# Sums of rank-times-key products on TensorE instead of VectorE, in the routing stage of a hybrid encoder layer

## The chip, the cores and the metric

The kernel runs on one core of one Trainium2 chip. The metric is the device time of one execution in microseconds (us); lower is better. The core has five engines with one queue each: TensorE (PE in the profile, its weight loads PEld), VectorE (DVE), ScalarE (ACT), GpSimd (POOL) and SyncE (SP), which here only issues DMAs. Each engine takes the instructions of its queue in order.

## The reference

One encoder layer on 512 tokens of width 1024. A mixer (a gated linear recurrence and a convolution side by side, then an output projection) is followed by PEER, a retrieval over 128 x 128 single-neuron experts; the change lies in PEER's routing alone:

```python
q = jnp.einsum("td,de->te", xt, w_q)                 # 8 heads x 2 halves x 128
s = jnp.einsum("thpc,hpkc->thpk", q, sub_keys)       # scores against 128 keys per half
s1, i1 = lax.top_k(s[:, :, 0], 16)
s2, i2 = lax.top_k(s[:, :, 1], 16)
cand_s = s1[..., :, None] + s2[..., None, :]         # 16 x 16 sums
cand_i = i1[..., :, None] * 128 + i2[..., None, :]
top_s, pos = lax.top_k(cand_s, 16)
idx = jnp.take_along_axis(cand_i, pos, axis=-1)
gate = jax.nn.softmax(top_s, axis=-1)
act = jax.nn.gelu(jnp.einsum("thkd,td->thk", expert_u[idx], xt))
out = jnp.einsum("thk,thkd->td", gate * act, expert_v[idx])
```

## The kernel before

After the mixer the kernel has four blocks of 128 tokens. Three of them are served densely: for all experts the products with `expert_u` are formed in 128 steps (`dense_u`, 24 matmuls of 384 columns each, lines 478 to 480), gates are scattered into a dense table, and the products with `expert_v` are summed in 128 steps (line 777). The fourth block gathers its experts' rows by indirect DMAs.

**The routing stage** lies between the mixer and the scatter of the gates, from about 270 to 480 us of the span. It loops over `hp`, 16 half heads. For each it runs a query (`query`, 24 matmuls of 512 columns, lines 587 to 589, evicted by ScalarE at line 591), the scores (line 602, evicted by ScalarE to a tile `s` at line 606) and, on VectorE, the sixteen best of each of the four token blocks (`rank`, by `best16`, lines 504 to 508). The queries run one step ahead. The list `US` says how many `dense_u` steps stand behind each `hp`: they fill TensorE while VectorE ranks; five of them stand behind the last one. Their weights are split into a high and a low part by ScalarE (line 108) and GpSimd or VectorE (line 110).

**`choose`** runs after `hp` = 3, 7 and 11 for two heads each and after 13 and 15 for one head each; with four token blocks that is m = 8 or m = 4. It converts the ranks' indices (`ii`, line 525, ScalarE), forms the candidate sums (line 529, GpSimd for m = 8), takes their sixteen best, turns the positions into the two indices j of the candidates (`pa`, `pf`, `pb`, lines 543 to 550), and looks up the keys' numbers without a gather: `eq` (line 554) is one where j equals a rank, [128, 2, 16 ranks, 16m] in bf16; line 557 multiplies it by the keys `ii`; four additions (three at line 560, the last at line 562) sum over the sixteen ranks into `key_d`. The gates go by GpSimd and ScalarE (lines 564 to 569).

**The order on each engine** is written when the program is built: the framework's scheduler places an instruction on its engine at the time at which it expects its inputs, by its own estimate of each duration, and takes the earlier one of the program first where several are ready. On the chip the engine then keeps that order, whatever comes late. After the last `choose` come `eidx` (line 614), transposes of the gates and keys (line 638) and the scatter (`hot`, `oa`, lines 661 and 665 on VectorE, `p_g`, line 671 on TensorE), in which VectorE also splits the weights of more `dense_u` steps.

Of the kernel before, what the change touches and what calls it, by code (L numbers as in the profile page):

```python
# [8 lines left out]
F32 = mybir.dt.float32  # L9
F32R = mybir.dt.float32r  # L10
BF16 = mybir.dt.bfloat16
# [7 lines left out]
P = 128  # L19
T = 512  # L20
D = 1024
NB = T // P
# [3 lines left out]
K = 16  # L26
NK = 128
# [33 lines left out]
def tile_kernel(ctx, tc, x, par, wi, bd, kd, mg, wo, wq, keys, u_rows, v_rows, u_t, v_t, fg, ffg, sel, out):  # L61
    nc = tc.nc
# [4 lines left out]
    ident = keep.tile([P, P], F32, name="ident")  # L67
# [4 lines left out]
    gate_d = keep.tile([P, H, NB, K], F32, name="gate_d")  # L72
    key_d = keep.tile([P, 2, H, NB, K], F32, name="key_d")
# [27 lines left out]
    def load(src):  # L101
        t = raw.tile([P, D], F32, name="raw_t")
        nc.sync.dma_start(t, src)
        return t

    def split(t, eng, pool=wp):
        hi = pool.tile([P, D], F32R, name="w_hi")
        nc.scalar.copy(hi, t)  # L108
        lo = pool.tile([P, D], F32R, name="w_lo")
        eng.tensor_sub(lo, t, f(hi))  # L110
        return hi, lo
# [33 lines left out]
    with ExitStack() as mx:  # L145
# [11 lines left out]
        with ExitStack() as m1:  # L157
# [169 lines left out]
            for n, eb in enumerate(order):  # L327
# [17 lines left out]
                kind, j = divmod(eb, 4)  # L345
# [47 lines left out]
            for b in range(NB):  # L393
                t = hb.tile([P, D], F32, name="h_t")
# [98 lines left out]
    for _ in range(4):  # L493
        t = gp.tile([P, D], F32, name="g_t")
# [4 lines left out]
    lp = ip.enter_context(tc.tile_pool(name="lp", bufs=1, side="right"))  # L499
    ioj = lp.tile([P, K, K * RM], BF16, name="ioj")  # L500
    nc.gpsimd.iota(ioj, pattern=[[1, K], [0, K * RM]], base=0, channel_multiplier=0, allow_small_or_imprecise_dtypes=True)

    def best16(val, idx, src, scratch):
        nc.vector.max(val[:, 0:8], src)
        nc.vector.max_index(idx[:, 0:8], val[:, 0:8], src)
        nc.vector.match_replace(scratch, val[:, 0:8], src, -3.4028235e38)
        nc.vector.max(val[:, 8:16], scratch)
        nc.vector.max_index(idx[:, 8:16], val[:, 8:16], scratch)

    def rank(rp, v, i, src):  # L510
        s2 = rp.tile([P, NK], F32, name="s2")
        best16(v, i, src, s2)

    def merge(t):
        return t.rearrange("p h b k -> p (h b) k")

    def choose(rp, v, i, g, keys_, h0, n):

        hh = slice(h0, h0 + n)
        vv = v[:, hh].rearrange("p h b t k -> p (h b) t k")  # L520
        m = vv.shape[1]
        shp = [P, m, K]

        ii = rp.tile([P, 2, K, m], BF16, name="ii")
        nc.scalar.copy(ii, i[:, hh].rearrange("p h b t k -> p t k (h b)"))

        cs = rp.tile([P, m, NCD], F32, name="cs", bufs=1)
        for lo_, ni, nj, c0 in ((0, 4, K, 0), (4, 12, 4, 64)):
            (nc.gpsimd if n > 1 else nc.vector).tensor_tensor(
                cs[:, :, c0:c0 + ni * nj].rearrange("p h (i j) -> p h i j", j=nj),  # L530
                vv[:, :, 0, lo_:lo_ + ni].unsqueeze(3).to_broadcast([P, m, ni, nj]),
                vv[:, :, 1, 0:nj].unsqueeze(2).to_broadcast([P, m, ni, nj]), op=ALU.add)
        ts = rp.tile(shp, F32, name="ts")
        pos = rp.tile(shp, U32, name="pos")
        for h in range(m):
            c2 = rp.tile([P, NCD], F32, name="c2")
            best16(ts[:, h], pos[:, h], cs[:, h], c2)

        pa = rp.tile([P, 5, m, K], U32, name="pa")
        for q, (op, arg) in enumerate(((ALU.logical_shift_right, 4), (ALU.logical_shift_right, 2),  # L540
                                       (ALU.bitwise_and, 15), (ALU.bitwise_and, 12),
                                       (ALU.logical_shift_right, 6))):
            nc.vector.tensor_scalar(pa[:, q], pos, arg, None, op0=op)
        pf = rp.tile([P, 5, m, K], F32, name="pf")
        nc.scalar.copy(pf, pa)
        pb = rp.tile([P, 2, K, m], BF16, name="pb")
        pbm = pb.rearrange("p t k m -> p t m k")
        nc.vector.scalar_tensor_tensor(pbm[:, 0], pf[:, 1], -12.0, pf[:, 0], op0=ALU.add, op1=ALU.max)
        nc.vector.tensor_mul(pf[:, 3], pf[:, 3], pf[:, 4])
        nc.vector.tensor_sub(pbm[:, 1], pf[:, 2], pf[:, 3])  # L550

        eq = rp.tile([P, 2, K, K * m], BF16, name="eq", bufs=1)
        shp2 = [P, 2, K, K * m]
        nc.vector.tensor_tensor(eq, pb.rearrange("p t k m -> p t (k m)").unsqueeze(2).to_broadcast(shp2),
                                ioj[:, :, 0:K * m].unsqueeze(1).to_broadcast(shp2), op=ALU.is_equal)
        e4 = eq.rearrange("p t j (k m) -> p (t j) k m", m=m)
        nc.vector.tensor_tensor(e4, e4, ii.rearrange("p t j m -> p (t j) m").unsqueeze(2).to_broadcast([P, 2 * K, K, m]),
                                op=ALU.mult)
        for w in (8, 4, 2):
            nc.vector.tensor_add(eq[:, :, 0:w], eq[:, :, 0:w], eq[:, :, w:2 * w])  # L560
        e1, e2 = (eq[:, :, w].rearrange("p t (k m) -> p t k m", m=m) for w in range(2))
        nc.vector.tensor_add(keys_[:, :, hh].rearrange("p t h b k -> p t k (h b)"), e1, e2)
        g = merge(g[:, hh])
        nc.gpsimd.tensor_tensor(g, ts, ts[:, :, 0:1].to_broadcast(shp), op=ALU.subtract)
        nc.scalar.activation(g, g, AF.Exp)
        den = rp.tile([P, m], F32, name="den")
        nc.vector.tensor_reduce(den, g, axis=AX.X, op=ALU.add)
        nc.vector.reciprocal(den, den)
        nc.gpsimd.tensor_tensor(g, g, den.unsqueeze(2).to_broadcast(shp), op=ALU.mult)

    with ExitStack() as rt:
        kp = rt.enter_context(tc.tile_pool(name="kp", bufs=1, side="right"))
        ky = kp.tile([P, 16, NK], F32, name="ky")
        nc.sync.dma_start(ky, keys)
        rp = rt.enter_context(tc.tile_pool(name="rp", bufs=2, side="right"))
        qp = rt.enter_context(tc.tile_pool(name="qp", bufs=4, side="right"))
        ps_q = rt.enter_context(tc.tile_pool(name="ps_q", bufs=3, space=PSUM))
        ps_s = rt.enter_context(tc.tile_pool(name="ps_s", bufs=3, space=PSUM))
        v16 = kp.tile([P, H, NB, 2, K], F32, name="v16")
        i16 = kp.tile([P, H, NB, 2, K], U32, name="i16")  # L580

        def query(hp):
            hi, lo = split(load(wq[hp].rearrange("p c e -> p (c e)")), nc.gpsimd)
            pq = ps_q.tile([P, T], F32, name="pq")
            for c in range(NC):
                cs = slice(c * P, (c + 1) * P)
                nc.tensor.matmul(pq, hi[:, cs], m_hi[:, c, :], start=(c == 0), stop=False)  # L587
                nc.tensor.matmul(pq, hi[:, cs], m_lo[:, c, :], start=False, stop=False)  # L588
                nc.tensor.matmul(pq, lo[:, cs], m_hi[:, c, :], start=False, stop=(c == NC - 1))  # L589
            q = qp.tile([P, T], F32, name="q", bufs=2)  # L590
            nc.scalar.activation(q, pq, AF.Copy)
            return q

        for _ in range(EARLY):
            dense_u(len(us), nc.gpsimd)
        qs = [query(0)]
        for hp in range(16):
            if 0 < hp < 15:
                qs.append(query(hp + 1))
            p = ps_s.tile([P, NB, NK], F32, name="p_s")  # L600
            for b in range(NB):
                nc.tensor.matmul(p[:, b, :], qs[hp][:, b * P:(b + 1) * P], ky[:, hp, :], start=True, stop=True)
            if hp == 0:
                qs.append(query(1))
            s = qp.tile([P, NB, NK], F32, name="s")
            nc.scalar.activation(s, p, AF.Copy)
            for b in range(NB):
                rank(rp, v16[:, hp // 2, b, hp % 2], i16[:, hp // 2, b, hp % 2], s[:, b])
            for _ in range(US[hp]):
                dense_u(len(us), nc.gpsimd)  # L610
            for h0, n in ((0, 2), (2, 2), (4, 2), (6, 1), (7, 1)):
                if hp == 2 * (h0 + n) - 1:
                    choose(rp, v16, i16, gate_d, key_d, h0, n)
        nc.vector.scalar_tensor_tensor(eidx, key_d[:, 0, :, DB], float(NK), key_d[:, 1, :, DB], op0=ALU.mult, op1=ALU.add)
    ip.close()

# [179 lines left out]
    for i in range(NK):  # L796
        n, o = divmod(i + AHEAD_W, GQ)
# [8 lines left out]
        if i < NK - LAST:  # L806
            w = ws.pop(i)
# [85 lines left out]
```

## Time and profile before

| what | value |
|---|---|
| median of three runs | 1543.34 us (1542.52 to 1551.58) |
| the profiled execution | 1543.64 us, span of its instructions 1541.5 us |
| mean granted clock of TensorE in it | 0.978 of 2.4 GHz |
| busy: TensorE, VectorE, ScalarE, GpSimd | 1467.7, 1232.5, 626.7, 625.4 us |

The span runs from the first to the last instruction. The rows below give times in us from the span's start. Matmuls overlap, so the busy time of TensorE is not its time at full rate; the distance from one start to the next is.

### The profile page before, as it was taken

How to read it: one execution, taken by the hardware profiler on the slowest of the kernel's cores; microseconds unless marked ns; L12 is line 12 of the kernel's file. 1: busy time of each engine (PE TensorE's matmuls, PEld its weight loads, DVE VectorE, ACT ScalarE, POOL GpSimd, SP SyncE). 2: the span in 40 equal slices, each digit the busy share in tenths (PEclk: the TensorE clock that was granted, in tenths of full speed). 3: DMA queues.
4: the chain of work that ended last, by engine and by line, in shares of the span. 5: the costliest groups of instructions: out<-in, count | busy, mean ns of one | idle time of the engine just before them, and what ended most of it. 6: DMA issues, size and time to landing. Idle time of an engine off the chain costs nothing.

```text
span 1541.5 us, 21654 instructions
## 1 busy us (share of the span) xinstructions
PE 1467.7 (95%) x7939; PEld 1289.4 (84%) x7939; DVE 1232.5 (80%) x2267; ACT 626.7 (41%) x926; POOL 625.4 (41%) x378
## 2 busy tenths in 40 slices
PE   5998698999988999999999999999999999999997
PEld 4766467899977899898999999999999999888886
DVE  5998556599999999937777777777777778788887
ACT  5457633344434555433333333333333333333333
POOL 1636542467551000124545545544454444443330
PEclk8999899999998999999999999999999999999999
DMA  6211313233222665588899898999989899889983
GB/s 238 82 55 58 134 69 123 97 109 98 92 95 100 226 212 213 212 259 311 290 334 318 327 340 289 342 305 332 326 318 326 301 348 319 304 310 339 331 290 135
DMA packets 137787, 358.69 MB, mean 233 GB/s; under 512 B 10064, under 2 KB 59472, under 8 KB 134352
## 3 DMA queue, kind: packets, MB, share of 16 engines
q1 hardware_dynamic: 100240, 222.03, 42.0%
q0 software_dynamic: 36864, 134.23, 24.2%
q8 instruction: 62, 1.02, 0.3%
q10 hardware_dynamic: 576, 1.05, 0.2%
q14 instruction: 45, 0.37, 0.1%
HBM read 327.91 MB, written 29.36 MB: 232 GB/s over the span
## 4 chain that ended last, share of the span: by engine, by line
PE 81%; DVE 13%; ACT 3%; issue 1%; POOL 1%; DMA 0%; SPq 0%; DVEq 0%; ACTq 0%; POOLq 0%
PE po L777 34%; PE p_e L478 10%; PE p_e L479 10%; PE p_e L480 10%; PE p_g L671 3%; DVE oa L665 2%; PE pq L587 2%; PE pq L588 2%; PE pq L589 2%; DVE hot L661 1%; PE pz L432 1%; PE pz L431 1%; PE pz L433 1%; PE pz L339 1%; PE pz L340 1%
## 5 line engine op out<-in xcount | busy, mean ns | idle before, releaser
L108 ACT CAST w_hi<-raw_t 128x1024 fp32r<-128x1024 f32 x302 | 315.9, 1050 | 411.6 <-PE p_e L479 266.8
L478 PE MATMUL p_e<-m_hi,w_hi 128*128 128x384 f32 x1024 | 350.7, 342 | 4.4 <-ACT w_e L487 3.5
L480 PE MATMUL p_e<-m_hi,w_lo 128*128 128x384 f32 x1024 | 347.3, 339 | 0.0
L479 PE MATMUL p_e<-m_lo,w_hi 128*128 128x384 f32 x1024 | 346.8, 339 | 0.3 <-DVE m_lo L142 0.3
L110 POOL TENSOR_TENSOR w_lo<-raw_t,w_hi 128x1024 fp32r<-128x1024 f32 x70 | 189.8, 2720 | 349.2 <-ACT w_hi L108 349.2
L110 DVE TENSOR_TENSOR w_lo<-raw_t,w_hi 128x1024 fp32r<-128x1024 f32 x232 | 280.9, 1222 | 13.6 <-ACT w_hi L108 13.4
L693 POOL DMA_INDIRECT g_t<-in_u_rows,eidx x128 | 197.4, 1543 | 214.0 <-DVE g_t L705 170.2
L693 POOL DMA_INDIRECT g_t<-in_v_rows,eidx x128 | 178.7, 1396 | 234.8 <-DVE acc L715 222.1
L777 PE MATMUL po<-w_hi,wt_hi 128*128 128x512 f32 x768 | 240.6, 393 | 0.0
L777 PE MATMUL po<-w_hi,wt_lo 128*128 128x512 f32 x768 | 239.5, 391 | 0.0
L777 PE MATMUL po<-w_lo,wt_hi 128*128 128x512 f32 x768 | 238.8, 390 | 0.0
L478 PEld LDWEIGHTS p_e<-m_hi,w_hi 128*128 128x128 f32 x1024 | 194.5, 190 | 8.3 <-ACT w_e L487 3.9
L479 PEld LDWEIGHTS p_e<-m_lo,w_hi 128*128 128x128 f32 x1024 | 194.5, 190 | 3.5 <-DVE m_lo L142 0.5
L480 PEld LDWEIGHTS p_e<-m_hi,w_lo 128*128 128x128 f32 x1024 | 194.5, 190 | 0.0
L777 PEld LDWEIGHTS po<-w_lo,wt_hi 128*128 128x128 f32 x768 | 144.2, 188 | 32.9
L777 PEld LDWEIGHTS po<-w_hi,wt_lo 128*128 128x128 f32 x768 | 144.3, 188 | 30.5
L705 DVE SCALAR_TENSOR_TENSOR g_t<-g_t,Xg 128x1024 f32<-128x1024 f32 x128 | 152.0, 1222 | 19.0 <-DMA g_t<-in_u_rows,eidx 18.8
L777 PEld LDWEIGHTS po<-w_hi,wt_hi 128*128 128x128 f32 x768 | 143.2, 188 | 24.9
L715 DVE SCALAR_TENSOR_TENSOR acc<-g_t,dots,acc 128x1024 f32<-128x1024 f32 x127 | 162.5, 1279 | 1.7 <-DMA g_t<-in_v_rows,eidx 1.7
L750 ACT CAST wt_hi<-w_f 128x384 fp32r<-128x384 f32 x69 | 35.4, 513 | 182.1 <-PE po L777 182.1
L752 DVE TENSOR_TENSOR wt_lo<-w_f,wt_hi 128x384 fp32r<-128x384 f32 x69 | 38.5, 558 | 73.7 <-ACT wt_hi L750 73.6
L665 DVE TENSOR_TENSOR oa<-hot,trb 128x1024 bf16<-128x1024 bf16 x144 | 92.3, 699 | 0.6
(220 smaller groups left out, 1906.2 us busy)
## 6 DMA issues: line engine op xcount, KB each, us to landing
raw_t<-in_u_t SPq DMA_DIRECT2D x128, 512.0 KB, 6.1
raw_t<-in_v_t SPq DMA_DIRECT2D x128, 512.0 KB, 6.1
scr_g<-stg SPq DMA_DIRECT2D x24, 1024.0 KB, 4.8
g_s<-scr_g SPq DMA_DIRECT2D x16, 1536.0 KB, 14.6
raw_t<-in_wi SPq DMA_DIRECT2D x16, 512.0 KB, 4.2
raw_t<-in_wq SPq DMA_DIRECT2D x16, 512.0 KB, 3.6
raw_t<-in_wo SPq DMA_DIRECT2D x8, 512.0 KB, 3.6
raw_t<-in_kd SPq DMA_DIRECT2D x6, 512.0 KB, 3.5
```

Source lines behind the costliest of these rows:

```text
L108: nc.scalar.copy(hi, t)
L110: eng.tensor_sub(lo, t, f(hi))
L478: nc.tensor.matmul(p, hi[:, cs], m_hi[:, c, :TD], start=(c == 0), stop=False)
L479: nc.tensor.matmul(p, hi[:, cs], m_lo[:, c, :TD], start=False, stop=False)
L480: nc.tensor.matmul(p, lo[:, cs], m_hi[:, c, :TD], start=False, stop=(c == NC - 1))
L665: nc.vector.tensor_tensor(oa[:, q], hot[:, 1], over(2 + q, 1), op=ALU.mult)
L671: nc.tensor.matmul(p[:, t, :], hot[:, 0, g, :, o], oa[:, q, g, :, o], start=(q == 0), stop=(q == 2))
L693: nc.gpsimd.indirect_dma_start(out=t, out_offset=None, in_=rows, in_offset=bass.IndirectOffsetOnAxis(ap=eidx[:, k // K, k % K:k % K + 1], ...
L705: nc.vector.scalar_tensor_tensor(t, t, 1.0, Xg, op0=ALU.mult, op1=ALU.mult, accum_out=dots[:, k:k + 1])
L715: nc.vector.scalar_tensor_tensor(acc, t, dots[:, k:k + 1], acc, op0=ALU.mult, op1=ALU.add)
L752: weighed.append(nc.vector.tensor_sub(wlo, flat(w), f(whi)))
L777: nc.tensor.matmul(po[b][hf], lhs[:, bs], rhs[:, hf * 512:(hf + 1) * 512], start=(i == 0 and n == 0), stop=(i == NK - 1 and n == 2))
```

## The change

The three halving additions and the last addition of `choose` go. In their place TensorE sums the sixteen products: sixteen matmuls with a bf16 unit matrix `identb` as one operand and `eq[:, :, j]`, two by 16m columns, as the other, accumulated in a tile of the scores' PSUM pool (`p_s`, three buffers), which VectorE then copies to `key_d`. `identb` is copied once from the f32 unit matrix by ScalarE. The conversion `ii` moves from ScalarE to VectorE. The tile `s` of evicted scores has six buffers instead of four.

```diff
+    identb = lp.tile([P, P], BF16, name="identb")
+    nc.scalar.copy(identb, ident)
...
-    def choose(rp, v, i, g, keys_, h0, n):
+    def choose(rp, ps, v, i, g, keys_, h0, n):
...
-        nc.scalar.copy(ii, i[:, hh].rearrange("p h b t k -> p t k (h b)"))
+        nc.vector.tensor_copy(ii, i[:, hh].rearrange("p h b t k -> p t k (h b)"))
...
-        for w in (8, 4, 2):
-            nc.vector.tensor_add(eq[:, :, 0:w], eq[:, :, 0:w], eq[:, :, w:2 * w])
-        e1, e2 = (eq[:, :, w].rearrange("p t (k m) -> p t k m", m=m) for w in range(2))
-        nc.vector.tensor_add(keys_[:, :, hh].rearrange("p t h b k -> p t k (h b)"), e1, e2)
+        pk = ps.tile([P, NB, NK], F32, name="p_s")[:, 0:2, 0:K * m]
+        for j in range(K):
+            nc.tensor.matmul(pk, identb, eq[:, :, j], start=(j == 0), stop=(j == K - 1))
+        nc.vector.tensor_copy(keys_[:, :, hh].rearrange("p t h b k -> p t k (h b)"), pk.rearrange("p t (k m) -> p t k m", m=m))
...
-            s = qp.tile([P, NB, NK], F32, name="s")
+            s = qp.tile([P, NB, NK], F32, name="s", bufs=6)
...
-                    choose(rp, v16, i16, gate_d, key_d, h0, n)
+                    choose(rp, ps_s, v16, i16, gate_d, key_d, h0, n)
```

## Rows read from the trace of the kernel before

**Rows 1.** The page, busy time of each engine, us, share of the span and instructions.

```profile
PE 1467.7 (95%) x7939; PEld 1289.4 (84%) x7939; DVE 1232.5 (80%) x2267; ACT 626.7 (41%) x926; POOL 625.4 (41%) x378
```

**Rows 2.** Chain of waits, 390 to 425 us: start, length, engine, tile, line.

```profile
396.80 0.89 PE p_s L602 x8
398.71 0.48 DVE v L504 x2
```

**Rows 3.** Windows: engines' busy us (instructions), granted clock, DMA share, GB/s.

```profile
420.00:440.00 20.00, 20.00 (x113) 18.67 (x112) 20.00 (x61) 3.47 (x5) 12.02 (x4) 1.00 0.32 106
440.00:450.00 10.00, 2.61 (x14) 2.29 (x13) 9.50 (x54) 5.97 (x10) 4.08 (x4) 0.85 0.16 52
```

**Rows 4.** Timeline of TensorE: start, length, line, shape, [idle before and its releaser].

```profile
411.13 0.39 PE L589 MATMUL pq<-m_hi,w_lo 128*128 128x512 f32 x1
...
437.44 0.42 PE L478 MATMUL p_e<-m_hi,w_hi 128*128 128x384 f32 x1
...
441.54 0.34 PE L480 MATMUL p_e<-m_hi,w_lo 128*128 128x384 f32 x1
449.27 2.07 PE L602 MATMUL p_s<-ky,q 128*128 128x128 f32 x8 [7.39 <-ACT q L591]
...
468.56 0.69 PE L478 MATMUL p_e<-m_hi,w_hi 128*128 128x384 f32 x1 [3.55 <-ACT w_e L487]
...
480.75 0.33 PE L638 MATMUL p_e<-ident,src 128*128 128x128 f32 x1 [0.95 <-ACT src L637]
```

**Rows 5.** Timeline of ScalarE, around the first, third and fourth choose.

```profile
311.20 0.59 ACT L591 ACTIVATE q<-pq 128x512 f32<-128x512 f32 x1
...
316.81 0.31 ACT L565 ACTIVATE gate_d<-gate_d 128x128 f32<-128x128 f32 x1 [3.23 <-POOL gate_d L564]
...
413.71 0.31 ACT L565 ACTIVATE gate_d<-gate_d 128x128 f32<-128x128 f32 x1 [5.03 <-POOL gate_d L564]
...
415.05 0.59 ACT L591 ACTIVATE q<-pq 128x512 f32<-128x512 f32 x1
...
441.62 0.42 ACT L525 CAST ii<-i 128x128 bf16<-128x128 uint32 x1 [13.12 <-DVE i L508]
...
448.63 0.59 ACT L591 ACTIVATE q<-pq 128x512 f32<-128x512 f32 x1
```

**Rows 6.** Groups by line on VectorE, 278 to 482 us: busy us, mean ns | idle before.

```profile
L560 DVE TENSOR_TENSOR eq<-eq 128x1024 bf16<-128x1024 bf16 (+3 forms) x15 | 29.4, 1959 | 0.1
...
L562 DVE TENSOR_TENSOR key_d<-eq 128x256 f32<-128x256 bf16 (+1 forms) x5 | 4.6, 922 | 0.0
```

**Rows 7.** Groups by line and shape on VectorE, 200 to 500 us: a read from PSUM.

```profile
L142 DVE TENSOR_TENSOR m_lo<-pt,m_hi 128x512 fp32r<-128x512 f32 x8 | 5.3, 688 | 5.6 <-ACT m_hi L141 5.6
```

**Rows 8.** Timeline of TensorE at the start of the scatter: bf16 matmuls of 128 columns.

```profile
489.78 1.55 PE L671 MATMUL p_g<-oa,hot 128*128 128x128 bf16 x24
```

**Rows 9.** Timeline of VectorE: three products of line 557, the last rank, `eidx`.

```profile
419.31 4.29 DVE L557 TENSOR_TENSOR eq<-eq,ii 128x4096 bf16<-128x4096 bf16 x1
...
449.91 3.27 DVE L557 TENSOR_TENSOR eq<-eq,ii 128x2048 bf16<-128x2048 bf16 x1
...
461.57 0.47 DVE L504 MAX8 v<-s 128x8 f32<-128x128 f32 x2
...
475.12 1.23 DVE L557 TENSOR_TENSOR eq<-eq,ii 128x2048 bf16<-128x2048 bf16 x1
...
480.32 0.29 DVE L614 SCALAR_TENSOR_TENSOR eidx<-key_d 128x128 int32<-128x128 f32 x1
```

**Rows 10.** Timeline of GpSimd beside the first of these products.

```profile
417.19 14.83 POOL L110 TENSOR_TENSOR w_lo<-raw_t,w_hi 128x1024 fp32r<-128x1024 f32 x4 [1.83 <-ACT w_hi L108]
```

**Rows 11.** Short windows after waits of TensorE, columns as in Rows 3.

```profile
468.00:469.00 1.00, 0.43 (x1) 0.44 (x2) 1.00 (x9) 0.98 (x3) 0.80 (x1) 0.50 0.00 0
...
474.00:475.00 1.00, 1.00 (x7) 1.00 (x6) 1.00 (x1) 0.99 (x3) 0.00 (x0) 0.86 0.00 0
...
485.00:490.00 5.00, 5.00 (x27) 4.52 (x26) 5.00 (x8) 0.56 (x1) 0.00 (x0) 0.71 0.13 49
```

## The prediction

> **What bounds the kernel now.** The page comes first: TensorE is busy for 95% of the span [rows 1], so a gain can only come from time in which it stands or runs at the lower of its two clocks. Next, windows over the routing stage [rows 3]. From 420 to 440 us TensorE and VectorE are both busy all the time, TensorE at clock 1.00. From 440 to 450 TensorE is busy for 2.6 us and VectorE for 9.5. Third, the chain of waits [rows 2]: it runs through TensorE up to the scores at 396.80 and from 398.71 through VectorE. So VectorE's savings before 396.80 are worth nothing, and from there they count only until TensorE is the later one again. Last, the timelines. TensorE finishes a `dense_u` step at about 441.7 and then stands for 7.39 us before the last scores, which wait for a query that ScalarE evicts at 448.63 [rows 4, 5]. ScalarE was held up by `ii`, for which it waited 13.12 us on VectorE's ranks [rows 5]. TensorE stands for another 3.55 us before 468.56 and reaches the first transpose of the scatter at 480.75 [rows 4]. The stage ends there, and from there on VectorE's and TensorE's work are what they were. The change is therefore priced by when this transpose comes.
>
> **What is removed and added on VectorE.** Off go 15 additions of line 560 and 5 of line 562, 29.4 + 4.6 = 34.0 us [rows 6]. Those of the last three chooses (four of eight heads) lie after 398.71: 17.0 us by heads. On comes a copy out of PSUM for each choose: the nearest row is 0.69 us for 512 columns in f32 [rows 7]; for 256 or 128 I take 0.4. `ii` lies between the 0.29 us of a conversion of 128 elements [rows 9] and the 0.92 us mean of line 562 [rows 6]; I take 0.5. The last three chooses thus add 2.7 us.
>
> **Edits with one answer.** `identb` is one small copy on ScalarE long before its first use. The two more `s` buffers I cost at nothing: a fifth set of scores would need one, and VectorE is never four half heads behind. The PSUM tile is shared with the scores, but three buffers serve scores that are a whole query or more apart, and a sum needs its one for a few us. VectorE's copy of the sum waits for TensorE, with the next half head's ranks behind it; VectorE has time for that once its additions are gone. `ii` off ScalarE takes away the 13.12 us block, and with it the 7.39 and the 3.55 us of TensorE; next late there is the exponential of line 565, which follows VectorE by GpSimd.
>
> **What is added on TensorE.** 24 bf16 matmuls of 128 columns took 1.40 us from the first to the last start, in the 1.55 us of the row [rows 8]: 0.058 each. Sixteen of 256 columns are then 1.9 us, sixteen of 128 columns 0.9. TensorE has no cover for them: three times 1.9 and twice 0.9 lie on its path.
>
> **The added wait.** TensorE's queue now holds matmuls that need VectorE's product of line 557. Behind them stand the next query, the scores on which VectorE's ranks wait, and the `dense_u` steps. They wait if the product comes later than the scheduler planned. How late VectorE runs against TensorE is read from ScalarE's order. ScalarE does not keep the program's order: at the first choose a later query's eviction, at 311.20, stands ahead of the exponential at 316.81 [rows 5]. At the third, the exponential (413.71) stands ahead of the later query's eviction (415.05) [rows 5], so the plan expected its input first. On the chip that query was done at 411.13 + 0.39 = 411.52 [rows 4], and the exponential could start at 413.71: 2.2 us late at the least. Then the product itself: 4.29 us beside four splits on GpSimd, against 2 x 1.23 us in half-size form with GpSimd still [rows 9, 10], 1.8 us more. I take the plan's duration for the undisturbed one, which no row shows. So a big choose makes TensorE wait 2.2 + 1.8 = 4.0 us. The bounds: nothing, if the plan leaves slack that this order does not show; and 5.03 us, all that ScalarE stood for the exponential [rows 5], plus 1.8 = 6.8. For the fourth choose I take the product's excess, 3.27 - 1.23 = 2.0 us; for the last none, as its product took 1.23 [rows 9].
>
> **TensorE's clock after a wait.** After the 3.55 us wait the granted clock is 0.50, the lower level, from 468 until within 474 to 475 [rows 4, 11]: 5.8 us at half rate cost 2.9. After shorter waits at 480.75 to 483.3 it is 0.71 from 485 to 490: 1.4 us lost [rows 4, 11]. I take 2.5 after a wait of 4.0 and 1.4 after one of 2.0.
>
> **A rule that speaks against the change.** The 7.39 us in row 449.27 show TensorE standing before scores with five `dense_u` steps behind them [rows 4]. The Trainium skill, "TensorE: Matmul & The Clock Gate", section "Part 2: What happens when you issue a matmul", says that matmuls stay in program order and only weight loads are pulled ahead. By that rule each late product holds the whole queue and the sum is the one below; if TensorE could pass the waiting matmuls, the first rival's would hold.
>
> **A second rule.** The product of 4.29 us stood beside GpSimd splits of 14.83 / 4 = 3.7 us [rows 9, 10]. The Trainium skill, "SBUF — State Buffer", section "Who interferes with whom", says that a VectorE instruction with two SBUF inputs and a GpSimd one that reads SBUF exclude each other for a whole instruction. By it the delay could be a whole split; the wait would be 2.2 + 3.7 = 5.9 us and the sum 5.7 us more. The measured 1.8 decides.
>
> **The sum.** Before, TensorE was free for the last scores at 441.7 had the query been there. Three big chooses move this by 3 x (1.9 + 4.0 + 2.5) = 25.2 us, the fourth by 0.9 + 2.0 + 1.4 = 4.3: 471.2. Then the scores (0.9 [rows 2]) and five steps of 24 matmuls; the step from 437.44 to 441.54 plus one distance is 4.3, less 0.1 for its slow first start is 4.2 [rows 4], five make 20.9; the last choose adds 0.9. The transpose comes at 493.9. VectorE is earlier: the last rank began at 461.57 and `eidx` stood at 480.32 [rows 9], 18.75 us; the removed and added work of the last choose about cancel, and with scores evicted at 472.9 it ends at 491.7. So 493.9 - 480.75 = 13.1 us later. On the profiled execution's 1543.64 us, which is 0.3 above the median, that is **1557 us**.
>
> **Rival 1: the products come in time.** No waits: 441.7 + 3 x 1.9 + 0.9 = 448.3, plus 0.9 + 20.9 + 0.9 = 22.7 is 471.0. VectorE's chain from 398.71 to 480.32 [rows 2, 9] is 81.6 us long; moved by two chooses (3.8), less 17.0, plus 2.7, it ends at 469.8. The transpose comes at 471.0, 9.7 us earlier: **1534 us**. For it speaks that TensorE's own delays could eat the lateness, and that VectorE, with less to do, starts each choose without arrears. Against it: VectorE waited for the scores at 398.71 [rows 2] and so had no arrears there either, yet was at least 2.2 us late 15 us on. It decides the sign: with waits and clock together under about 10 us over the four chooses, the change is not slower.
>
> **Rival 2: the waits are long.** At 6.8 us, with 2.9 for the clock, three big chooses cost 34.8 and the fourth 5.8; the transpose comes at 505.0, 24 us later: **1568 us**.
>
> **Rival 3: the matmuls stand at their program place.** Before, queries, scores and `dense_u` steps run on TensorE in program order throughout the stage. If the sixteen matmuls did too, they would follow the steps of their own half head, and TensorE would wait for nearly the whole choose. From the scores at 396.80 + 0.89 VectorE needs until 419.31 + 4.29 = 423.6, and TensorE has two steps, 8.4 us: 17.6 us of wait three times, some 8 on the fourth: 3 x (17.6 + 1.9 + 2.9) + 11.8 = 79 on 441.7, and 22.7: 63 us later, **1606 us**. The first choose on ScalarE, where a later query's eviction stands ahead [rows 5], speaks against it.
>
> **Rival 4: VectorE's time is freed for nothing.** If the conversion and copy on VectorE meet GpSimd's splits as line 560 did, they cost up to the 1.96 us mean of that line each [rows 6], 11.8 us over the last three chooses in place of 2.7. VectorE's chain without waits of TensorE would end at 478.9 and the time be **1542 us**: near no change, and counted with rival 1's band.
>
> **How the numbers follow.** Forecast, waits of some 2.5 to 6 us: 0.5. Rival 1, with the band up to break-even and rival 4: 0.33. Rival 2: 0.1. Rival 3: 0.03. A new plan that gains beyond rival 1: 0.04. About 1%, 15.4 us, is what the runs, 9 us apart among three, can tell from no change. Faster by over 1% needs more than rival 1 gives: the 0.04 and 0.03 of its band, 0.07. The forecast lies 13.1 us up, so just under half of it and all of rivals 2 and 3 are slower by over 1%: 0.36; the rest, 0.57. The range reaches from rival 1 with a little below to past rival 2: 1531 to 1571 us.
>
> **What would show it.** In the profile after: line 560's additions gone and VectorE idle between scores from 340 us on; gaps of TensorE before the unit-matrix matmuls, released by VectorE's product, three of 3 to 5 us with clock 0.50 behind them; no 13 us of ScalarE before an index conversion, no 7 us of TensorE before the last scores; the first transpose at about 494. Without such gaps, and with the transpose near 471, rival 1 holds. Wrong would make me, above all, a plan that puts these matmuls later than I infer, or steps moved in the rest of the kernel.

## The result and the profile after

The changed kernel takes **1565.07 us** (median of four, 1563.74 to 1572.59) where the kernel before takes 1543.63 us beside it (1542.52 to 1551.58): ratio 1.0141, 95% interval 1.0119 to 1.0163, so 1.4% slower. Forecast were 1557 us and a range of 1531 to 1571. The profiled execution's span is 1561.9 us, 20.4 more than before.

The page first, engines' busy times as in [rows 1]:

```profile
PE 1475.1 (94%) x8019; PEld 1292.9 (83%) x8019; DVE 1214.1 (78%) x2257; ACT 625.4 (40%) x922; POOL 618.6 (40%) x378
```

TensorE has 80 instructions and 7.4 us more, VectorE 18.4 us less, and the span is longer: TensorE's standing must have grown. The timeline of TensorE after shows where: all the unit-matrix matmuls (line 564) that waited by over a microsecond, and the first transpose of the scatter (line 641, before 638), columns as in [rows 4]:

```profile
326.66 3.59 PE L564 MATMUL p_s<-eq,identb 128*128 128x256 bf16 x16 [5.26 <-DVE eq L560]
...
384.33 3.60 PE L564 MATMUL p_s<-eq,identb 128*128 128x256 bf16 x16 [7.31 <-DVE eq L560]
...
446.32 3.59 PE L564 MATMUL p_s<-eq,identb 128*128 128x256 bf16 x16 [7.31 <-DVE eq L560]
...
474.82 1.89 PE L564 MATMUL p_s<-eq,identb 128*128 128x128 bf16 x16 [4.53 <-DVE eq L560]
...
504.10 0.33 PE L641 MATMUL p_e<-ident,src 128*128 128x128 f32 x1 [0.67 <-ACT src L640]
```

Each time TensorE stood for VectorE's product (line 560, before 557): 24.41 us in four waits. The transpose comes at 504.10 in place of 480.75 [rows 4], 23.35 us later. After it 1057.8 us are left of the span, against 1060.75 before.

The chain of waits after, columns as in [rows 2], has VectorE's product ahead of TensorE's sum and scores already at the first choose, where before it ran through TensorE up to 396.80:

```profile
322.29 4.32 DVE eq L560
...
326.66 3.59 PE p_s L564 x16
330.25 2.12 PE p_s L605 x16
```

Windows over the stage, columns as in [rows 3]. First after, the last two rows being the 8 us behind the first and the fourth wait; then before, where TensorE never stood from 320 to 440, with the 8 us behind its waits of 7.39 and 3.55 us:

```profile
320.00:340.00 20.00, 14.74 (x84) 13.29 (x84) 15.01 (x57) 5.71 (x9) 10.10 (x3) 0.83 0.18 56
340.00:360.00 20.00, 20.00 (x109) 18.18 (x108) 9.49 (x62) 6.16 (x10) 9.59 (x4) 1.00 0.31 108
...
400.00:420.00 20.00, 20.00 (x107) 18.05 (x106) 5.71 (x38) 6.94 (x10) 9.44 (x5) 1.00 0.31 107
...
326.66:334.66 8.00, 8.00 (x47) 7.01 (x48) 3.11 (x18) 1.57 (x3) 2.14 (x1) 0.74 0.25 91
...
474.82:482.82 8.00, 8.00 (x55) 8.00 (x56) 4.39 (x29) 2.90 (x3) 1.14 (x1) 0.83 0.17 63
```

```profile
320.00:340.00 20.00, 20.00 (x114) 18.87 (x113) 19.97 (x40) 8.07 (x12) 17.75 (x6) 1.00 0.32 106
...
449.27:457.27 8.00, 8.00 (x37) 8.00 (x38) 7.93 (x11) 4.30 (x6) 6.14 (x2) 0.72 0.29 94
...
468.56:476.56 8.00, 8.00 (x31) 8.00 (x32) 7.57 (x35) 5.51 (x7) 2.59 (x3) 0.64 0.19 66
```

The freed time of VectorE is there: 9.49 busy of 20 us from 340, 5.71 from 400. TensorE made nothing of it. The 8 us behind the first wait ran at a mean clock of 0.74, so 8 x 0.26 = 2.1 us were lost.

The timeline of VectorE after, at the first choose, and two later rows that tell of its idle time:

```profile
319.96 2.29 DVE L557 TENSOR_TENSOR eq<-pb,ioj 128x4096 bf16<-128x4096 bf16 x1
322.29 4.31 DVE L560 TENSOR_TENSOR eq<-eq,ii 128x4096 bf16<-128x4096 bf16 x1
330.29 0.59 DVE L565 COPY key_d<-p_s 128x256 f32<-128x256 f32 x1 [3.69 <-PE p_s L564]
332.14 0.49 DVE L507 MAX8 v<-s 128x8 f32<-128x128 f32 x2 [1.26 <-ACT s L609]
...
346.71 0.49 DVE L507 MAX8 v<-s 128x8 f32<-128x128 f32 x2 [4.86 <-ACT s L609]
...
408.70 0.49 DVE L507 MAX8 v<-s 128x8 f32<-128x128 f32 x2 [8.73 <-ACT s L609]
```

In a choose the two engines take turns: TensorE stands until the product ends at 326.60, then VectorE until the sum is done, then until the next scores are evicted (line 609). Those scores stand behind the sum on TensorE. Next, the timeline of GpSimd at the first two chooses, splits of weights that lie beside the product, and at the second beside the compare of line 557 too:

```profile
321.10 7.70 POOL L110 TENSOR_TENSOR w_lo<-raw_t,w_hi 128x1024 fp32r<-128x1024 f32 x2 [2.65 <-ACT w_hi L108]
...
375.39 6.73 POOL L110 TENSOR_TENSOR w_lo<-raw_t,w_hi 128x1024 fp32r<-128x1024 f32 x2 [1.34 <-ACT w_hi L108]
```

VectorE's groups by line and shape from 278 to 505 us (busy us, mean ns, idle before):

```profile
L560 DVE TENSOR_TENSOR eq<-eq,ii 128x4096 bf16<-128x4096 bf16 x3 | 12.9, 4311 | 0.1
...
L557 DVE TENSOR_TENSOR eq<-pb,ioj 128x4096 bf16<-128x4096 bf16 x3 | 11.0, 3656 | 0.1
...
L528 DVE CAST ii<-i 128x256 bf16<-128x256 uint32 x3 | 2.9, 961 | 0.1
...
L565 DVE COPY key_d<-p_s 128x256 f32<-128x256 f32 x3 | 1.8, 590 | 11.1 <-PE p_s L564 11.1
```

### The profile page after: what moved, and what is told of

It is laid out like the page before. It is cut to its first block, busy times and chain, and to the rows that moved or that the text cites. A ratio compares the mean times of both kernels' runs of the same rounds, so it can differ in the third digit from the quotient of the medians.

```text
span 1561.9 us, 21803 instructions
## 1 busy us (share of the span) xinstructions
PE 1475.1 (94%) x8019; PEld 1292.9 (83%) x8019; DVE 1214.1 (78%) x2257; ACT 625.4 (40%) x922; POOL 618.6 (40%) x378
## 4 chain that ended last, share of the span: by engine, by line
PE 80%; DVE 15%; ACT 3%; issue 1%; POOL 0%; DMA 0%; SPq 0%; DVEq 0%; ACTq 0%; POOLq 0%
PE po L780 33%; PE p_e L478 10%; PE p_e L480 10%; PE p_e L479 10%; PE p_g L674 3%; DVE oa L668 2%; DVE hot L664 1%; PE pq L590 1%; PE pq L592 1%; PE pq L591 1%; DVE eq L560 1%; PE pz L432 1%; PE pz L431 1%; PE pz L433 1%; PE p_s L605 1%
## 5 line engine op out<-in xcount | busy, mean ns | idle before, releaser
L110 POOL TENSOR_TENSOR w_lo<-raw_t,w_hi 128x1024 fp32r<-128x1024 f32 x70 | 180.4, 2584 | 379.3 <-ACT w_hi L108 379.2
```

## The experiments

Two theories stood after these rows. **Theory A**: TensorE's queue holds the sum at a place that the plan found right and the chip's VectorE reaches late; everything behind it waits. **Theory B**: the sum's tile is one of the scores' three buffers and the framework hands these out in program order, so the next scores are kept behind the sum, which starves VectorE and makes its products late in the first place. No run shows the times that the plan held: "late" means here that TensorE reached the sum's place before VectorE had the product, and whether VectorE is slower than planned or TensorE faster isn't told apart. Every ratio is against the kernel before, run on the same chip in the same session (1543.69 to 1544.19 us in the three sessions).

**own_psum: a PSUM pool of the sum's own**

```diff
-        pk = ps.tile([P, NB, NK], F32, name="p_s")[:, 0:2, 0:K * m]
+        pk = ps.tile([P, NB, NK], F32, name="p_k")[:, 0:2, 0:K * m]
...
-        ps_s = rt.enter_context(tc.tile_pool(name="ps_s", bufs=3, space=PSUM))
+        ps_s = rt.enter_context(tc.tile_pool(name="ps_s", bufs=2, space=PSUM))
+        ps_k = rt.enter_context(tc.tile_pool(name="ps_k", bufs=1, space=PSUM))
```

> The sums get a PSUM buffer of their own, taken from the scores' three (now two); all else as in the change. Theory A (TensorE's queue waits for VectorE's product, 24.4 us in four waits, and runs at the lower clock after each): the scores come on time again, but the sums stand no later in TensorE's queue, so the waits stay at 5 to 9 us each and the time at 1560 to 1570 us. Theory B (the shared tile holds back the next scores, VectorE starves, and that makes the loss): VectorE has its ranks to do while the sum is late, and the time falls by 10 us or more, to 1555 us or less.

Measured: 1564.15 us (1562.22 to 1565.02), ratio 1.0118 [1.0079, 1.0158]. The timeline of TensorE in it, two of the four waits:

```profile
327.53 3.39 PE L564 MATMUL p_k<-eq,identb 128*128 128x256 bf16 x16 [6.04 <-DVE eq L560]
...
441.45 3.57 PE L564 MATMUL p_k<-eq,identb 128*128 128x256 bf16 x16 [5.26 <-DVE eq L560]
```

With 5.28 and 3.54 us for the others the four are 20.1 us. The transpose comes at 498.78, 5.3 us earlier than in the changed kernel, but the rest of the span is 3.8 us longer (1061.6 against 1057.8), and the time is not told apart from the changed kernel's. Theory B falls as the cause of the loss; at most some 4 us of the waits hang on it.

**no_wait: the sixteen matmuls with an operand that is always there**

```diff
-            nc.tensor.matmul(pk, identb, eq[:, :, j], start=(j == 0), stop=(j == K - 1))
+            nc.tensor.matmul(pk, identb, ioj[:, j, 0:K * m].unsqueeze(1).to_broadcast([P, 2, K * m]), start=(j == 0), stop=(j == K - 1))
```

> The same sixteen matmuls, of the same size and into the same shared tile, but they read the constant table instead of the products, so they wait for nothing of VectorE; the products are still formed. Left out: the keys' numbers (all become 120, so gathers and scatter run with wrong keys). Theory A: the four waits and their clock dips go, the sums' own 7 to 8 us stay; the first transpose of the scatter comes at about 471 to 475 us and the time is 1533 to 1540 us. Theory C (the matmuls themselves, or VectorE's conversion and copy, are what costs): 1555 us or more.

Measured: 1541.99 us (1540.74 to 1546.9, ten), ratio 0.9988 [0.9971, 1.0005]. The same matmuls on the same engine, without the wait, are 23 us cheaper: theory C falls. Their place is not the same, though: since they need nothing of VectorE, the plan puts the first sum right behind the `dense_u` step of its own half head, at 304.65, the place of the prediction's rival 3, where in the change TensorE comes to it at 321.40. So this run prices the sums, the copies and the conversion, not the place. And the transpose was expected at 471 to 475 and came at 478.14. The timeline of TensorE shows what was left:

```profile
470.56 0.54 PE L478 MATMUL p_e<-m_hi,w_hi 128*128 128x384 f32 x1 [4.27 <-ACT w_e L487]
...
478.14 0.33 PE L641 MATMUL p_e<-ident,src 128*128 128x128 f32 x1 [0.67 <-ACT src L640]
```

ScalarE, on whose `w_e` TensorE stood for 4.27 us, had itself waited at the exponential at 467.60, 6.99 us for GpSimd's `gate_d`. With `ii` off ScalarE, it still waited for the chain that VectorE feeds.

**ii_alone: the kernel before with the conversion on VectorE**

```diff
-        nc.scalar.copy(ii, i[:, hh].rearrange("p h b t k -> p t k (h b)"))
+        nc.vector.tensor_copy(ii, i[:, hh].rearrange("p h b t k -> p t k (h b)"))
```

> The kernel before with only the conversion of the ranks moved to VectorE. Theory A: ScalarE no longer blocks the last query, TensorE's 7.4 and 3.6 us of standing go, but VectorE's chain is what ends the stage there and gets 3 to 5 us longer; the time is 1542 to 1549 us, no measurable change. If ScalarE's block was the bound, 1530 to 1537 us.

Measured: 1546.49 us (1545.38 to 1550.89, ten), ratio 1.0012 [0.9997, 1.0028]. The timelines of ScalarE and TensorE in it:

```profile
448.73 0.26 ACT L565 ACTIVATE gate_d<-gate_d 128x64 f32<-128x64 f32 x1 [15.07 <-POOL gate_d L564]
```

```profile
451.33 2.08 PE L602 MATMUL p_s<-ky,q 128*128 128x128 f32 x8 [9.74 <-ACT q L591]
...
476.92 0.69 PE L478 MATMUL p_e<-m_hi,w_hi 128*128 128x384 f32 x1 [5.65 <-ACT w_e L487]
```

Before, ScalarE stood 13.12 us before `ii` [rows 5]; now it stands 15.07 before the exponential, two steps further down the same chain from VectorE's ranks, and TensorE's 7.39 and 3.55 us [rows 4] have become 9.74 and 5.65. Moving the conversion frees nothing.

**late_sum: own pool, and the sum given out later in the program**

The sum and its copy become a function that the routing loop calls two half heads after its choose (one for the fourth, at once for the last), behind that half head's `dense_u` steps:

```diff
+        def total():
+            pk = ps.tile([P, NB, NK], F32, name="p_k")[:, 0:2, 0:K * m]
+            for j in range(K):
+                nc.tensor.matmul(pk, identb, eq[:, :, j], start=(j == 0), stop=(j == K - 1))
...
-                    choose(rp, ps_s, v16, i16, gate_d, key_d, h0, n)
+                    totals.append((min(hp + 2, 15) if n > 1 else hp + 1, choose(rp, ps_k, v16, i16, gate_d, key_d, h0, n)))
+            while totals and (totals[0][0] <= hp or hp == 15):
+                totals.pop(0)[1]()
```

> As own_psum, and the matmuls of the sum are issued two half heads later in the program (one for the fourth choose), behind the dense steps there, when VectorE's product has long been done; the last sum as in the change. Theory A: no waits, 1532 to 1540 us, faster than both kernels. Theory B: the same, since the tile is its own. Theory C: 1555 us or more.

Measured: **1536.32 us** (1535.56 to 1538.48, seven), ratio 0.9942 [0.9918, 0.9965]: 28.8 us less than the changed kernel with the same instructions, and 0.6% faster than the kernel before. Its timeline of TensorE, and a window (columns as in [rows 3]):

```profile
330.01 1.92 PE L573 MATMUL p_k<-eq,identb 128*128 128x256 bf16 x16
...
448.62 1.07 PE L573 MATMUL p_k<-eq,identb 128*128 128x128 bf16 x16 [1.49 <-DVE eq L560]
...
474.26 0.33 PE L650 MATMUL p_e<-ident,src 128*128 128x128 f32 x1 [0.67 <-ACT src L649]
```

```profile
320.00:340.00 20.00, 20.00 (x120) 18.55 (x119) 15.78 (x61) 8.16 (x12) 15.41 (x6) 1.00 0.33 106
```

There is no wait before the sums of 256 columns, the clock is at 1.00, and the transpose comes at 474.26. The fourth sum, one half head later, still waits for 1.49 us. On TensorE the first sum stands at 330.01, only 8.6 us behind the 321.40 at which TensorE began to wait for it in the change, and 2.1 us behind the end of its product (323.65 + 4.22 on VectorE). The pool differs here too; whether the place alone does it is the next run.

**late_shared: late_sum with the tile back in the scores' three buffers**

```diff
-            pk = ps.tile([P, NB, NK], F32, name="p_k")[:, 0:2, 0:K * m]
+            pk = ps.tile([P, NB, NK], F32, name="p_s")[:, 0:2, 0:K * m]
```

> As late_sum, but the sums' tile is again one of the scores' three buffers, as in the change. If only the place of the matmuls in TensorE's queue counts, the time is that of late_sum, 1534 to 1538 us; if the shared tile costs by itself, 1541 us or more.

Measured: 1536.7 us (1536.38 to 1537.03), ratio 0.9954 [0.9938, 0.9969], as late_sum. Against the changed kernel only the place differs, and it is worth 28.4 us; the shared tile costs nothing that can be measured.

**quiet_pool: the changed kernel without GpSimd's splits in the stage**

```diff
-            eng.tensor_sub(lo, t, f(hi))
+        if quiet:
+            nc.gpsimd.memset(f(lo), 0.0)
+        else:
+            eng.tensor_sub(lo, t, f(hi))
```

> The change, but in the routing stage GpSimd clears the low parts of the weights instead of subtracting, so it reads nothing from SBUF there; the matmuls on the low parts still run. Left out: the low parts of the weights in queries and dense steps of this stage. Theory A1 (about half of each wait is GpSimd's splits stretching VectorE's conversion, comparison and product): the big products take 2.3 us instead of 4.3, the four waits fall from 24.4 us to 8 to 14, the time to 1548 to 1556 us. Theory A2 (VectorE is late against the plan for another reason): waits stay above 18 us, 1558 us or more.

Measured: 1550.87 us (1548.53 to 1552.34), ratio 1.0038 [1.0023, 1.0052]. The timelines of TensorE and VectorE in it:

```profile
325.38 2.79 PE L569 MATMUL p_s<-eq,identb 128*128 128x256 bf16 x16 [4.25 <-DVE eq L565]
...
463.44 1.07 PE L569 MATMUL p_s<-eq,identb 128*128 128x128 bf16 x16 [1.82 <-DVE eq L565]
```

```profile
374.99 2.29 DVE L562 TENSOR_TENSOR eq<-pb,ioj 128x4096 bf16<-128x4096 bf16 x1
377.32 2.29 DVE L565 TENSOR_TENSOR eq<-eq,ii 128x4096 bf16<-128x4096 bf16 x1
```

The product takes 2.29 us with GpSimd idle beside it and 4.31 beside its splits. The waits are 4.25, 4.23, 4.24 and 1.82, 14.5 in sum, just over what was expected, and 9.9 us less than in the change.

But 4.2 us is not how late a big choose is undisturbed, for GpSimd isn't quiet in this run: it clears the low parts, and it forms candidate sums and gates as before. Its clearings fall elsewhere. The timelines of VectorE (at the first and the second choose) and GpSimd (at the first) in quiet_pool, and the row of `pa` at the first choose of the changed kernel:

```profile
307.62 0.46 DVE L512 MAX8 ts<-cs 128x8 f32<-128x112 f32 x2 [0.96 <-POOL cs L537]
...
370.97 1.51 DVE L551 TENSOR_SCALAR pa<-pos 128x128 uint32<-128x128 uint32 x5
```

```profile
316.70 0.95 POOL L113 MEMSET w_lo<- 128x1024 f32 x1
```

```profile
316.70 0.77 DVE L546 TENSOR_SCALAR pa<-pos 128x128 uint32<-128x128 uint32 x5
```

In each big choose `pa` takes 1.51 us beside a clearing, where it takes 0.77 in the change. VectorE also starts on the candidates later: it stands 0.96 us for GpSimd's second candidate sum, which comes behind a clearing, and starts 6.43 us after the choose's last ranks began (301.19), where the change needs 5.96 (301.67 to 307.63). These 1.2 us are the edit's own, so some 3.0 us of a big choose's wait are there undisturbed. For the first choose this adds up: 3.0 and the product's 2.0 are 5.0, beside 5.26. The splits' share of the 24.4 us is then nearer 9.9 + 3 x 1.2 = 13.5 than 10.

**ii_back and s_four: the changed kernel with `ii` on ScalarE, and with four `s` buffers**

```diff
-        nc.vector.tensor_copy(ii, i[:, hh].rearrange("p h b t k -> p t k (h b)"))
+        nc.scalar.copy(ii, i[:, hh].rearrange("p h b t k -> p t k (h b)"))
```

> The change with the conversion of the ranks back on ScalarE. Theory A: VectorE gets to the product up to 1 us earlier in each big choose, the waits shrink by 0.5 to 1 us each, 1560 to 1566 us, within what can't be told from the change. If the move to VectorE was what freed TensorE's tail, it comes back slower, 1570 us or more.

```diff
-            s = qp.tile([P, NB, NK], F32, name="s", bufs=6)
+            s = qp.tile([P, NB, NK], F32, name="s")
```

> The change with four buffers for the evicted scores instead of six. Both theories: nothing waits for one of them, the order on TensorE is the same, 1563 to 1567 us.

Measured: 1566.63 us (1564.87 to 1567.22), ratio 1.0138 [1.0121, 1.0155], and 1563.92 us (1563.03 to 1566.34), ratio 1.0127 [1.011, 1.0144]. Neither is told apart from the change. In ii_back the waits are 5.13, 7.18, 7.17 and 3.93 us, at the big chooses only 0.13 less, where 0.5 to 1 was expected: with the conversion gone, VectorE stands 0.78 us for GpSimd's candidate sum instead. In its timeline of ScalarE no 13 us stand before the conversion, although it is on ScalarE:

```profile
464.63 0.43 ACT L528 CAST ii<-i 128x128 bf16<-128x128 uint32 x1 [2.93 <-DVE i L511]
```

With TensorE standing at every sum, VectorE can have caught up by then; the next run bears on that.

**late_ii_back: late_sum with `ii` on ScalarE** (the edit of ii_back on late_sum)

> As late_sum, with the conversion of the ranks on ScalarE. If the conversion on VectorE costs the stage's end (0.96 us beside a split), 1534 to 1537 us, no worse than late_sum; if ScalarE's wait for the ranks matters once VectorE is less busy, 1538 to 1545 us.

Measured: 1540.83 us (1539.37 to 1544.12), ratio 0.9975 [0.9964, 0.9986], above every run of late_sum. The timelines of TensorE and ScalarE in it:

```profile
453.35 1.89 PE L573 MATMUL p_k<-eq,identb 128*128 128x128 bf16 x16 [3.59 <-DVE eq L560]
```

```profile
439.57 0.43 ACT L528 CAST ii<-i 128x128 bf16<-128x128 uint32 x1 [4.95 <-DVE i L511]
```

Without the long waits, the conversion on ScalarE does hold that engine, here for 4.95 us, and the fourth sum waits for 3.59 where in late_sum it waits for 1.49. So moving `ii` is worth some 4 us (4.5 by the times of two sessions; the transpose comes 3.7 us later counted from the stage's first rank), but only once the waits are gone.

**late_last3: late_sum for the last three chooses, VectorE's additions in the first two**

```diff
+            if h0 < 4:
+                for w in (8, 4, 2):
+                    nc.vector.tensor_add(eq[:, :, 0:w], eq[:, :, 0:w], eq[:, :, w:2 * w])
```

> As late_sum for the last three chooses; the first two keep their additions on VectorE, as before. If TensorE alone ends the stage once nothing waits, two sums of 1.9 us less bring 3 to 4 us: 1531 to 1534 us. If VectorE is the bound again with those additions back, 1537 us or more.

Measured: 1535.94 us (1532.07 to 1536.58), ratio 0.9942 [0.9928, 0.9955]: not told apart from late_sum, against the 1531 to 1534 us expected. In its profile the transpose stands at 473.04, 1.2 us earlier, though the stage's first rank began 1.5 us later (279.98 against 278.50). Counted from that rank, the transpose comes 2.7 us earlier, so VectorE's additions in the first two chooses cost little there; the time does not show it.

## Why the prediction was right or wrong

**What bounds, and where the change is priced: right.** The transpose moved by 23.35 us and the span by 20.4. The 3.0 us that the rest of the span gives back were forecast as nothing. They make the time look better forecast (8 us off) than the transpose was (10.2 us off), and that is luck; their cause was not tested (in own_psum the rest is 1560.4 - 498.78 = 1061.6 us, near the 1060.75 of before).

**VectorE's savings buy nothing: right.** The copies took 0.59 and 0.37 us, forecast 0.4. `ii` took 0.96 and 0.27 us, forecast 0.5. VectorE stood between scores from 340 us on, as forecast, and TensorE set the end.

**The sums' own time: right.** In late_sum, at full clock, 1.92 and 1.07 us, forecast 1.9 and 0.9.

**The clock: right.** The 8 us behind each wait ran at 0.74, 0.72, 0.75 and 0.83: 7.7 us lost, where 3 x 2.5 + 1.4 = 8.9 were forecast.

**The added wait: the mechanism right, the size wrong.** This is the step that failed. Forecast were 3 x 4.0 + 2.0 = 14.0 us, measured 24.41: 5.26, 7.31, 7.31 and 4.53. The prediction's own sum with the measured terms put in is 441.7 + 24.4 + 7.7 + 3 x 1.92 + 1.07 + 22.7 = 503.3, beside 504.10 in the trace. So hardly any other term is missing, and the 10.4 us of wait more, less 1.2 of clock, are the miss. Three parts made the term too small. The 2.2 us of lateness were read from the exponential as "at the least" and then used as the value: by quiet_pool they are some 3.0. The stretch beside GpSimd was charged once, to the product (forecast 1.8, measured 4.31 - 2.29 = 2.0); at the second and third choose the splits fall on the compare of line 557 too, 4.34 us in place of 2.29, as much as the 2.05 us between the waits of 5.26 and 7.31. In the kernel before all three compares took 2.29, and in quiet_pool too. At the fourth choose the product's excess was forecast rightly (3.24 - 1.23 = 2.0), but no lateness was charged, and quiet_pool waits there too, for 1.82 us; VectorE's candidate sum (line 532) took 1.64 us beside a split in the change and 0.35 in quiet_pool. Nearer in size, at the transpose, was rival 2 with waits of 6.8 us: 505.0, beside 504.10. Where the 3.0 us of lateness come from stays open.

**"`ii` off ScalarE takes away the 13.12 us block, and with it the 7.39 and the 3.55 us of TensorE": the standing did go, for another reason.** ii_alone moves `ii` and keeps the block, ii_back leaves `ii` and loses it. What ended it in the change were VectorE's freed time and the new waits, in which it caught up. The two were not told apart, but without the long waits, in late_ii_back, ScalarE stands for the ranks again, for 4.95 us. The same error made rival 1 too good: without waits its transpose was put at 471.0; no_wait came at 478.14, with 4.27 us of TensorE behind ScalarE's exponential. Without its waits the change as it stands is near no change (1542 us). Why late_sum keeps only 0.95 us of that standing and comes at 474.26 is not settled: the two have different plans.

**"Three buffers serve scores that are a whole query or more apart": wrong, at no cost that can be measured.** The scores of the next half head stand behind the sum, and VectorE idles for them. own_psum and late_shared show that this doesn't set the time.

**The two rules that were weighed.** That matmuls keep program order (the Trainium skill, "TensorE: Matmul & The Clock Gate", section "Part 2: What happens when you issue a matmul") agrees with the trace: at 326.66 the scores, queries and steps behind the waiting sum waited too, and late_shared gains 28.4 us by the place alone. The other (the Trainium skill, "SBUF — State Buffer", section "Who interferes with whom"), by which such a VectorE instruction and GpSimd's reads exclude each other, had been priced at a whole split of 3.7 us. The measured delay of 2.0 us is within one undisturbed split (2.40 us on GpSimd at 454.84). The 3.7 was itself stretched, as the two splits of 7.70 us are, and so was no measure of it.

## What to carry to other kernels

Work moved to an engine that takes its queue in order brings its wait with it: ask what stands behind it, and give it a place in the program late enough for the lateness that the trace shows, not for the one that the plan holds; here the place, 8.6 us further down the queue, was worth 28.4 us and the instructions themselves next to nothing. A lateness read as "at the least" is a bound, and all instructions of the late engine beside the contending one are to be charged, not only the one seen stretched before. An instruction that an engine waits in is not what holds it up: follow the chain on before moving it.

## What the hardware showed that was not expected

A compare of [128, 4096] in bf16 took 2.29 us in all three chooses before and 4.34 in two of them after, when two GpSimd splits had come to lie beside it. In quiet_pool, without the splits, all three took 2.29 again. At the first choose after, the compare began at 319.96, before the split at 321.10, and took 2.29 too.

The conversion of 256 numbers from uint32 to bf16 on VectorE took 0.96 us in the changed kernel and 0.40 in quiet_pool, and it is GpSimd's candidate sum that lay beside it, not a split. In the change that sum started first (306.39 to 307.45; the conversion 306.75 to 307.71). In quiet_pool the conversion started 0.05 us ahead of it, at 306.26, and the sum took 1.27 us in place of 1.06. The other two big chooses show the same: here the one of the two that started second was the one stretched. The stretch of the conversion cost next to nothing, as the ranking of the candidates needs that sum in any case; in ii_back VectorE stands 0.78 us for it.

Two GpSimd splits beside VectorE's product took 7.70 us, where a single one elsewhere took 2.40: both sides pay.
